# Dilated attention in pairs of query blocks, with the probabilities divided on VectorE and a new order of the first output products

## The chip, the cores and the metric

The kernel runs on one core of a Trainium2 chip. TensorE (PE) multiplies matrices out of SBUF into PSUM, VectorE (DVE), ScalarE (ACT) and GpSimd (POOL) work on tiles, and SyncE (SP) issues the DMA transfers. Each engine has its own queue, works it off in order, and waits on semaphores for the others. The metric is the device time of one execution in microseconds (us); less is better.

## What is computed

One layer of a hybrid decoder, for 1024 positions of width 1024, all in float32. Cut to what matters here:

```python
h = rmsnorm(x, norm1_w)
proj = h @ w_in                       # 3592 columns: q, k, v, gate z, b, a; then q, k, v of mixer B
...
o_a = gated_delta_rule(qa, ka, va, g, beta)        # mixer A: 4 heads of 128
o_a = rmsnorm(o_a, gdn_norm_w) * jax.nn.silu(z)
o_b = dilated_attention(qb, kb, vb)                # mixer B: 8 heads of 64
x = x + jnp.concatenate([o_a, o_b], axis=-1) @ w_out
h = rmsnorm(x, norm2_w)
u = causal_dwconv(h @ w_up, ffn_conv_w)
x = x + (jax.nn.silu(gate) * up) @ w_down
return rmsnorm(x, final_norm_w)
```

`dilated_attention` has three branches, (window, dilation) = (128, 1), (512, 4), (2048, 16). In each, position t sees t, t-d, t-2d, ... back to t-window. The branches are merged by their softmax denominators, which is the same as one softmax over all the keys of the three branches, a key counting as often as it is in a branch.

## The kernel before, in words

**Layout.** Activations lie transposed: features on the partitions, the 1024 positions on the free axis, in two halves of 512. Float32 products are made of three products in fp32r, high by high, high by low and low by high (`mm3`, L184; `split`, L190, makes the high part on ScalarE and the low part, the difference, on VectorE). A weight tile of 128 columns (`weight`, L194) is loaded, and split into `whi` and `wlo`.

**Stages.** The input projection comes as *dense* columns (`dense`, L462): 128 output columns each, two halves, 24 products of 128x512 a half, then an evacuation out of PSUM that also applies the norm (`xr`, or `aqkv` for mixer B, which is parked in DRAM as `apark`). The list `DENSE` (L37) gives their order. In between run mixer A's chunked recurrence and, from 313 us on, mixer B's attention. Then follow the output projection (`out_proj`, L1003), the convolutional MLP, and the last norm; those after the output projection are not touched.

**Who sets the order.** Every stage is a Python generator, and a planner (`Weave`, L42) runs them all while the program is being built. It keeps a modelled time for TensorE (`pe`) and for each other engine, with an estimate for each operation: `mm(..., us)` (L176) gives a product's time, an `Engine` (L117) works out its own from the tile's size, and `account` (L74) notes when a tile will be ready. A generator yields how long it still has to wait (`need`, L91: the latest `ready` of its tiles minus `pe`, plus a slack), and the planner goes on with the most urgent stream (lowest level number) whose wait is over. Attention is at level 5, the output projection at 8, the dense columns at 9: a dense product goes to TensorE whenever attention's operands are, in the model, not ready. TensorE's order is pinned in the order in which the planner issues; the order of the other engines' queues is left to the tile scheduler. So an estimate moves instructions but has no time itself.

**Attention** (`attention`, L839) takes four pairs of heads (`pi` 0 to 3), two halves of 512 queries each (`hh`), four blocks of 128 queries in each half. Both heads of a pair go side by side, as they have 64 rows each. `att_load` (L816) loads q, k and v; `att_values` (L822) transposes v into `vn` (positions on the partitions) and makes `vc` from it by 16 DMA transfers, in which the positions are sorted by their class modulo 4. For one block of queries:

- `scores` (L856): two products of the *band*, 128 queries by up to 256 keys (the block and the one before it), and eight of the *window*, in tiles of 32 queries of one class by the keys of that class, 32 a block. The softmax rows are 256 wide for block 0 of a pair, 384 for blocks 1 to 3, 512 for blocks 4 to 7. Then, on the other engines: a masked reduction to the negative maximum (`sm<-ps,mk`, VectorE), `exp` with its sum (`sm<-sm,mx`, ScalarE), the reciprocal of the sums (`mx<-mx`, VectorE), and the division, a multiplication by it (`sm<-sm,mx` again, ScalarE).
- `turn` (L887): transposes of the probabilities through PSUM. The band's part is copied to `pt` (VectorE), the window's part to `pb` (ScalarE).
- `values` (L900): products of `vn` and `pt` into the half's bank `po`.
- `merge_classes` (L908), once in a half: products of `vc` and the `pb` of all four blocks into the same bank. `give` (L920) then copies `po` out; the halves go to DRAM (`mixer`), the last one stays in SBUF as `oT`.

`advance` (L935) puts blocks into a pipe. With block i's scores issued, it issues the values of block i-2 (and the classes and `give` when that was a half's last) and then the turn of block i-1.

PSUM has 8 banks: the tags `hf`, `asc`, `ch` and `atr` have two each (`bank`, L226). Scores take `asc`, turns `atr`, `po` is in `ch`, dense products in `hf`. Tiles with a tag ending in `*` take turns between two tags (`A`, L156): `dv*` means `dv` and `dw`, two buffers each, where the `sm` lie; `t1` has three buffers, for `pt` (and two tiles of other stages, L305 and L618).

**The output projection.** `mixer_splits` (L978) loads the eight head blocks of the mixers' output (four of mixer A, already gated in SBUF; four of mixer B, from DRAM) and splits them into `ohi` and `olo`; the tag of the loaded tile, `ev`, has two buffers and is shared with the gate of the last dense columns. `out_proj` (L1003) has the output tiles in the order of `MORDER`; for the first two, in four banks, it goes over the head blocks outside and the two tiles inside; from the third on a tile is one run of 8 head blocks a half. Two weight tiles are held at a time.

Of the kernel before, what the change touches and what calls it, by code (L numbers as in the profile page):

```python
# [15 lines left out]
P = 128  # L16
# [17 lines left out]
HOP = 0.5  # L34
ASLACK = 1.2
MSLACK = 1.5
MGAP = 0.6  # L37
DENSE = ([("k", 3), ("a", 0, 0), ("a", 0, 1)] + [(c, h) for h in range(4) for c in "qv"] + [("a", 0, 2)]
         + [("a", p, i) for p in (1, 2, 3) for i in range(3)] + [("z", h) for h in range(4)])
# [96 lines left out]
def hybrid_layer(tc, I, out):  # L136
# [14 lines left out]
    def tile_(pool, shape, dt, name, tag, bufs):  # L151
        return wv.slot(pool.tile(list(shape), dt, name=name, tag=tag, bufs=bufs), tag, bufs)
# [73 lines left out]
    def bank(tag, name="ps"):  # L226
        return tile_(pp_, (P, 512), F32, name, tag, 2)
# [10 lines left out]
    def v8(t):  # L238
        return t.rearrange("p (c t) -> p c t", c=NCH)
# [62 lines left out]
    dtb = const("dtb", [P, H], bass.AP(tensor=I["dt_bias"].tensor, offset=I["dt_bias"].offset, ap=[[0, P], [1, H]]))  # L302
    gw2 = const("gw2", [P, 1])
    ve.tensor_scalar(gw2, gnw, 0.5, None, op0=OP.mult)
    wba = tile_(sp, [P, KT, 32], F32, "wba", "t1", 3)  # L305
    po_.memset(wba, 0.0)
    sy.dma_start(wba[:, :, :8], I["wba"])
    ve.tensor_tensor(wba[:, :, :8], wba[:, :, :8], n1[:, :, None].to_broadcast([P, KT, 8]), op=OP.mult)
# [302 lines left out]
    def forward_sub():  # L611

        mt_t = A("mt", "go")
        sy.dma_start(mt_t, mdram.rearrange("h p f -> (h p) f"))
        mt = mt_t.rearrange("p (j i) -> p j i", j=32)
        xi_t = A("xi", "go")
        xi = xi_t.rearrange("p (i c) -> p i c", i=32)
        tmp = tile_(sp, [P, 256], F32, "tmp", "t1", 3)  # L618
# [203 lines left out]
    def att_values(vT):  # L822

        vn, vc = A("vn", "kt"), A("vc", "kt")
        for hh in range(2):
            pt = yield from next_bank("atr", vT, slack=ASLACK * (hh == 0))
            for c in range(4):
                i = 4 * hh + c
                tp(pt[:, c * P:(c + 1) * P], vT[:, i * P:(i + 1) * P])
            ac.activation(vn[:, half(hh)], pt, AF.Copy)  # L830
        for c in range(4):
            for n in range(4):
                sy.dma_start(vc[32 * n:32 * n + 32].rearrange("u (c b d) -> u c b d", c=4, b=2)[:, c],
                             vn[32 * c:32 * c + 32].rearrange("u (b n d) -> u n b d", b=2, n=4)[:, n])
        return vn, vc

    HALVES = (slice(0, 64), slice(64, 128))

    def attention():  # L839
# [13 lines left out]
            t = mks[i]  # L853
            return bass.AP(tensor=t.tensor, offset=t.offset + o, ap=[t.ap[0], [step, m], [1, w]]), m

        def scores(it):  # L856
            n, q, k, nb = it["n"], it["q"], it["k"], it["nb"]
            pss = [bank("asc") for _ in range(2)]
            yield wv.need(*pss, q, k)
            k0 = max(n - 1, 0) * P  # L860
            n1_, n2_ = (n + 1) * P - k0, P * nb
            wd = n1_ + n2_
            for e, er in enumerate(HALVES):
                mm(pss[e][:, :n1_], q[er, n * P:(n + 1) * P], k[er, k0:k0 + n1_], 0.0009 * n1_)
            for c in range(4):
                o = slice(32 * c, 32 * c + 32)
                for e, er in enumerate(HALVES):
                    mm(pss[e][o, n1_:wd].rearrange("p (n u) -> p n u", u=32), q[er, n * P + 32 * c:n * P + 32 * c + 32],
                       by_block(k)[er, :4 * nb, c, :], 0.00025 * n2_, tile_position=(64 * e, 32 * c))
            sm = A("sm", "dv*", shape=(P, 2, 512))  # L870
            mx = tile_(sp, [P, 4], F32, "mx", "mx", 4)
            mn, den = mx[:, :2], mx[:, 2:]
            mv, m = mask(n)
            for e in range(2):
                ve.tensor_tensor_reduce(out=sm[:, e, :wd].rearrange("p (a b) -> p a b", a=m),
                                        in0=pss[e][:, :wd].rearrange("p (a b) -> p a b", a=m), in1=mv, scale=-0.125,
                                        scalar=-NEG, op0=OP.add, op1=OP.min, accum_out=mn[:, e:e + 1])
            for e in range(2):
                ac.activation(sm[:, e, :wd], sm[:, e, :wd], AF.Exp, bias=mn[:, e:e + 1], scale=-1.0,
                              accum_out=den[:, e:e + 1])  # L880

            ve.reciprocal(den, den)
            for e in range(2):
                ac.activation(sm[:, e, :wd], sm[:, e, :wd], AF.Copy, scale=den[:, e:e + 1])
            it.update(sm=sm, wd=wd, n1=n1_, k0=k0)

        def turn(it):  # L887
            sm, wd, n1_ = it["sm"], it["wd"], it["n1"]
            it["pt"] = []
            for e in range(2):  # L890
                pt = tile_(sp, [P, 256], F32, "pt", "t1", 3)
                it["pt"].append(pt)
                pp = bank("atr")
                yield wv.need(pp, sm)
                for i in range(wd // P):
                    tp(pp[:, i * P:(i + 1) * P], sm[:, e, i * P:(i + 1) * P])
                ve.tensor_copy(pt[:, :n1_], pp[:, :n1_])
                ac.activation(it["pb"][e][:, it["u"]].rearrange("p b t -> p (b t)"), pp[:, n1_:wd], AF.Copy)

        def values(it):  # L900
            u = it["u"]
            yield wv.need(it["po"], *it["pt"])
            for i in range(it["n1"] // P):
                for e, er in enumerate(HALVES):
                    mm(it["po"][er, u * P:(u + 1) * P], v8(it["vn"])[:, it["k0"] // P + i, er],
                       it["pt"][e][:, i * P:(i + 1) * P], 0.12, u == 0 and i == 0, False, skip_group_check=True)

        def merge_classes(g):  # L908
            vcv = g["vc"].rearrange("p (c b d) -> p c b d", c=4, b=2)
            po, nb = g["po"], g["nb"]  # L910
            yield wv.need(*g["pb"])
            for c in range(4):
                for b in range(nb):
                    for e in range(2):
                        er = slice(64 * e, 64 * e + 64)
                        mm(po[er].rearrange("p (u t) -> p u t", u=4)[:, :, 32 * c:32 * c + 32],
                           vcv[:, c, b, er], g["pb"][e][:, :, b, 32 * c:32 * c + 32], 0.14,
                           False, c == 3 and b == nb - 1, skip_group_check=True)
# [13 lines left out]

        pipe = []

        def advance(it):  # L935
            if it is not None:
                yield from scores(it)
            pipe.insert(0, it)
            if len(pipe) > 2:
                done = pipe.pop()  # L940
                if done is not None:
                    yield from values(done)
                    if done["u"] == 3:
                        yield from merge_classes(done["g"])
                        give(done["g"])
            if len(pipe) > 1 and pipe[1] is not None:
                yield from turn(pipe[1])

        for pi in range(4):
            q, k, vn, vc = cur  # L950
            for hh in range(2):
# [9 lines left out]
                for u in range(4):  # L961
                    yield from advance(dict(n=4 * hh + u, u=u, q=q, k=k, vn=vn, nb=nb, po=po, pb=pb, g=g))
            if pi < 3:
                cur = qkv[:2] + (yield from att_values(qkv[2]))
        for _ in range(2):
            yield from advance(None)


    ots = {}
# [33 lines left out]
    def out_proj():  # L1003
# [2 lines left out]
        yield from wv.until("last group")  # L1006
        yield from wv.until("residual")
        pts = {m: [bank(t) for _ in range(2)] for m, t in zip(MORDER, ("hf", "ch"))}
        for k in range(8):
            yield from wv.until(("ot", k))  # L1010
            for m, w in zip(MORDER, ws):
                for h in range(2):
                    yield wv.need(pts[m][h], *w, *ots[k])
                    mm3(pts[m][h], [t[:, k, :] for t in w], [t[:, half(h)] for t in ots[k]], k == 0, k == 7)
        for j, m in enumerate(MORDER):
            w = ws.pop(0)
            for h in range(2):
# [468 lines left out]
```

## Time and profile before

| | us |
|---|---|
| median of 3 runs (lowest, highest) | 1257.34 (1256.65, 1259.51) |
| profiled execution | 1259.56 |
| span in its trace, first to last instruction | 1257.8 |
| granted TensorE clock, mean | 0.993 of full speed |

The stretch that the change touches, from the trace's table by windows (busy us of each engine, with the number of instructions):

| from : to, us | PE | DVE | ACT | POOL | DMA share |
|---|---|---|---|---|---|
| 315.8 : 515.8, attention | 199.5 (1754) | 107.8 (268) | 117.1 (278) | 0 | 0.25 |
| 515.8 : 538.3, first two output tiles | 22.4 (97) | 12.6 (16) | 9.2 (13) | 0 | 0.42 |

Busy time of PE is the time in which at least one matmul is under way, and matmuls are pipelined: a stretch that is filled may still hold time in which no column moves. So stalls of TensorE are read here from the starts of its instructions. In the tables and views, a name such as `sm<-ps,mk` is the tile written and the tiles read, L132 is the line of the helper through which every operation of VectorE, ScalarE and GpSimd goes, L177 that of `mm` and L181 that of the transposes; x64 is the number of instructions in a group. A tile's shape is partitions by elements.

Attention's own work on its tiles, from the trace's view of one tile (ns; lowest, median, highest):

| instruction | engine | count | ns |
|---|---|---|---|
| `sm<-ps,mk` reduction, two forms | DVE | 32 and 32 | 398, 687, 701 and 540, 558, 692 |
| `sm<-sm,mx`, 64 `exp` and 64 divisions | ACT | 128 | 496, 664, 731 |
| `ps<-ident,sm` transposes | PE | 216 | 270, 273, 330 |
| `pt<-ps` copies | DVE | 64 | 270, 421, 436 |
| `ps<-pt,vn` value products | PE | 240 | 272, 273, 323 |

### The profile page before, as it was taken

What the parts mean: (1) busy time and instruction counts of PE and PEld (TensorE: products, weight loads), DVE (VectorE), ACT (ScalarE), POOL (GpSimd) and SP (SyncE); (2) the same over time, 40 slices, a digit from 0 to 9 for tenths busy, and PEclk for the clock granted to TensorE, in tenths of its full rate; (3) what the DMA queues carried; (4) which work ended last, traced back from release to release, by engine and by line L of the source; (5) the groups of instructions that cost most, each with busy time, mean ns of one, the idle gap of its engine ahead of it and who ended that gap; (6) DMA issues with size and microseconds to landing.
All of it is one profiled execution on the core that took longest, in us unless ns stands there. A gap on an engine that the chain in (4) does not pass through costs nothing.

```text
span 1257.8 us, 18320 instructions
## 1 busy us (share of the span) xinstructions
PE 1233.0 (98%) x7040; PEld 1002.1 (80%) x7040; DVE 936.0 (74%) x1462; ACT 621.8 (49%) x1179; POOL 47.8 (4%) x34
## 2 busy tenths in 40 slices
PE   9989999999999999999999999999999999999996
PEld 7768887888676767878788888888888888787886
DVE  7566975563555455676798888888988989899875
ACT  7374444462757374465554454544544454343451
POOL 0021110022000000000000000000000000000000
PEclk9989999999999999999999999999999999999998
DMA  6313244255223420454312313223223298545523
GB/s 228 100 57 94 85 116 137 101 160 206 96 78 100 140 63 26 126 179 139 118 51 101 92 59 101 85 67 101 79 73 101 68 353 290 167 138 198 192 85 134
DMA packets 81974, 153.52 MB, mean 122 GB/s; under 512 B 21824, under 2 KB 32736, under 8 KB 81888
## 3 DMA queue, kind: packets, MB, share of 16 engines
q1 hardware_dynamic: 81888, 152.37, 37.1%
q8 instruction: 55, 0.90, 0.3%
q14 instruction: 31, 0.25, 0.1%
HBM read 114.31 MB, written 35.93 MB: 119 GB/s over the span
## 4 chain that ended last, share of the span: by engine, by line
PE 84%; DVE 7%; DMA 4%; ACT 2%; issue 2%; SPq 0%; POOL 0%; POOLq 0%; DVEq 0%; ACTq 0%
PE ps L177 44%; PE pa L177 18%; PE pc L177 9%; PE dw L177 8%; PE ps L181 4%; DMA wd<-in_wd 3%; DVE pr L132 2%; DVE x1h L132 1%; DVE wd L132 1%; ACT dec L132 1%; DVE kT L132 1%; PE warm L177 1%; DMA wst<-in_wu 0%; DVE r L132 0%; DVE xr L132 0%
## 5 line engine op out<-in xcount | busy, mean ns | idle before, releaser
L177 PE MATMUL dw<-pr 128*128 128x512 f32 (+1 forms) x984 | 213.3, 377 | 2.8 <-DVE x1h L132 2.8
L177 PEld LDWEIGHTS dw<-pr 128*128 128x128 f32 x984 | 176.1, 188 | 38.9 <-DVE x1h L132 4.9
L177 PE MATMUL ps<-xhi,whi 128*128 128x512 f32 x448 | 186.5, 416 | 0.0
L177 PE MATMUL ps<-xhi,wlo 128*128 128x512 f32 x448 | 175.8, 392 | 0.0
L177 PE MATMUL ps<-xlo,whi 128*128 128x512 f32 x448 | 175.3, 391 | 0.0
L177 PE MATMUL pa<-T,pair 128*128 128x512 f32 x528 | 127.1, 389 | 0.6 <-ACT u L132 0.6
L177 PEld LDWEIGHTS pa<-T,pair 128*128 128x128 f32 x528 | 99.0, 188 | 21.1 <-ACT u L132 0.7
L177 PEld LDWEIGHTS ps<-xhi,whi 128*128 128x128 f32 x448 | 84.6, 189 | 19.9 <-issue 6.0
L177 PEld LDWEIGHTS ps<-xhi,wlo 128*128 128x128 f32 x448 | 84.4, 188 | 18.5
L177 PEld LDWEIGHTS ps<-xlo,whi 128*128 128x128 f32 x448 | 84.8, 189 | 13.5
L132 ACT ACTIVATE sm<-sm,mx 128x512 f32<-128x512 f32 (+2 forms) x128 | 79.9, 651 | 23.0 <-DVE mx L132 23.0
L132 ACT ACTIVATE u<-pa 128x512 f32<-128x512 f32 x44 | 26.4, 600 | 110.5 <-PE pa L177 110.5
L132 DVE SCALAR_TENSOR_TENSOR y<-xu,fcw,y 128x1023 f32<-128x1023 f32 (+1 forms) x44 | 56.3, 1281 | 25.7 <-ACT y L132 25.7
L132 ACT ACTIVATE whi<-wst 128x1024 fp32r<-128x1024 f32 (+2 forms) x38 | 38.7, 1017 | 70.4 <-PE ps L177 63.0
L177 PE MATMUL pc<-B,pair 128*128 128x512 f32 x264 | 63.4, 389 | 0.0
L177 PE MATMUL pa<-B,A 128*128 128x512 f32 x264 | 63.4, 389 | 0.0
L177 PE MATMUL pc<-T,S 128*128 128x512 f32 x264 | 63.4, 389 | 0.0
L177 PE MATMUL pa<-T,S 128*128 128x512 f32 x264 | 63.4, 389 | 0.0
L132 ACT ACTIVATE pr<-wd 128x1024 fp32r<-128x1024 f32 x33 | 35.0, 1061 | 55.0 <-DVE wd L132 36.5
L132 DVE TENSOR_TENSOR wst<-wst 128x512 f32<-128x512 f32 x88 | 60.5, 687 | 0.7
L177 PE MATMUL ps<-B,pair 128*128 128x512 f32 x252 | 60.5, 389 | 0.0
L177 PEld LDWEIGHTS pc<-B,pair 128*128 128x128 f32 x264 | 49.6, 188 | 10.3
(230 smaller groups left out, 2279.8 us busy)
## 6 DMA issues: line engine op xcount, KB each, us to landing
wst<-in_wu SPq DMA_DIRECT2D x44, 512.0 KB, 3.7
wd<-in_wd SPq DMA_DIRECT2D x44, 512.0 KB, 4.3
wst<-in_wi SPq DMA_DIRECT2D x25, 512.0 KB, 3.7
upark<-y SPq DMA_DIRECT2D x22, 512.0 KB, 3.7
apark<-aqkv SPq DMA_DIRECT2D x12, 512.0 KB, 2.8
r<-upark SPq DMA_DIRECT2D x11, 512.0 KB, 7.6
r<-upark SPq DMA_DIRECT2D x22, 256.0 KB, 6.7
wa<-in_wd SPq DMA_DIRECT2D x22, 256.0 KB, 2.9
```

Source lines behind the costliest of these rows:

```text
L132: return getattr(eng, op)(*a, **kw)
L177: tc.stamp_issue_order_token(nc.tensor.matmul(dst, lhs, rhs, start=start, stop=stop, **kw).ins, TOKEN)
L181: tc.stamp_issue_order_token(nc.tensor.transpose(dst, src, ident).ins, TOKEN)
```

## The change

1. **Pairs of blocks.** `scores`, `turn` and `values` take two blocks at a time. The first block's scores and turns use the banks `asc`, the second's `atr`. Within `scores`, the band products of both blocks come first, then the window products of both; the same operations as before on the other engines are put in a function of their own, `softmax`, once a block. The pipe is one pair deep: `advance` issues the turn of the pair before, the scores of the new pair, the values of the pair before, and its classes. Values and classes are offered 0.5 us before the model has their operands ready (`PSLACK`), turns 0.2 us after (`TSLACK`); some estimates of products are lower. The four `pt` of a pair are one tile in `dv*`.
2. **`vc` estimate.** The planner takes `vc` as ready 6.0 us after `vn`, whatever it had summed up for the 16 transfers.
3. **Division on VectorE.** `tensor_scalar` by the reciprocal on VectorE in the place of ScalarE's activation: 64 instructions from one queue to the other.
4. **First output tiles by heads.** For the first two output tiles, the head blocks 0 to 6 of the first tile, then those of the second, then block 7 of both.
5. **`t1`** keeps one buffer, for the two tiles of other stages.

TensorE's program has the same 6002 instructions in both kernels.

```diff
+PSLACK = 0.5
+TSLACK = 0.2, 0.2
...
-    wba = tile_(sp, [P, KT, 32], F32, "wba", "t1", 3)
+    wba = tile_(sp, [P, KT, 32], F32, "wba", "t1", 1)
...
+        wv.ready[vc.tensor.name] = max(wv.pe, wv.ready[vn.tensor.name]) + 6.0
         return vn, vc
...
-        def scores(it):
+        def scores(pair):
+            for it, tag in zip(pair, ("asc", "atr")):
...
+                it["ps"] = [bank(tag) for _ in range(2)]
+            yield wv.need(*pair[0]["ps"], *pair[1]["ps"], pair[0]["q"], pair[0]["k"])
+            for it in pair:
+                n, k0, n1_ = it["n"], it["k0"], it["n1"]
                 for e, er in enumerate(HALVES):
+                    mm(it["ps"][e][:, :n1_], it["q"][er, n * P:(n + 1) * P], it["k"][er, k0:k0 + n1_], 0.00085 * n1_)
+            for it in pair:
+                n, n1_, wd = it["n"], it["n1"], it["wd"]
+                for c in range(4):
+                    o = slice(32 * c, 32 * c + 32)
+                    for e, er in enumerate(HALVES):
+                        mm(it["ps"][e][o, n1_:wd].rearrange("p (n u) -> p n u", u=32),
+                           it["q"][er, n * P + 32 * c:n * P + 32 * c + 32], by_block(it["k"])[er, :4 * it["nb"], c, :],
+                           0.00022 * (wd - n1_), tile_position=(64 * e, 32 * c))
+                softmax(it)
...
             ve.reciprocal(den, den)
             for e in range(2):
-                ac.activation(sm[:, e, :wd], sm[:, e, :wd], AF.Copy, scale=den[:, e:e + 1])
...
+                ve.tensor_scalar(sm[:, e, :wd], sm[:, e, :wd], den[:, e:e + 1], None, op0=OP.mult)
+
+        def turn(pair):
+            pts = A("pt", "dv*", shape=(P, 4, 256))
+            for b, (it, tag) in enumerate(zip(pair, ("asc", "atr"))):
...
+                    pt = pts[:, 2 * b + e, :]
+                    it["pt"].append(pt)
+                    pp = bank(tag)
+                    yield wv.need(pp, sm, slack=TSLACK[b])
+                    for i in range(wd // P):
+                        tp(pp[:, i * P:(i + 1) * P], sm[:, e, i * P:(i + 1) * P])
+                    ve.tensor_copy(pt[:, :n1_], pp[:, :n1_])
...
+        def values(pair):
+            yield wv.need(pair[0]["po"], *pair[0]["pt"], slack=-PSLACK)
+            for it in pair:
+                u = it["u"]
+                for i in range(it["n1"] // P):
                     for e, er in enumerate(HALVES):
...
+                           it["pt"][e][:, i * P:(i + 1) * P], 0.11, u == 0 and i == 0, False, skip_group_check=True)
...
-            yield wv.need(*g["pb"])
+            yield wv.need(*g["pb"], slack=-PSLACK)
...
-        def advance(it):
...
-            if len(pipe) > 2:
-                done = pipe.pop()
...
-            if len(pipe) > 1 and pipe[1] is not None:
-                yield from turn(pipe[1])
+        def advance(pair):
+            done = pipe.pop() if pipe else None
+            if done is not None:
+                yield from turn(done)
+            if pair is not None:
+                yield from scores(pair)
+                pipe.append(pair)
+            if done is not None:
+                yield from values(done)
+                if done[1]["u"] == 3:
+                    yield from merge_classes(done[0]["g"])
+                    give(done[0]["g"])
...
-        for k in range(8):
+
+        for k, j in [(k, j) for j in range(2) for k in range(7)] + [(7, 0), (7, 1)]:
             yield from wv.until(("ot", k))
-            for m, w in zip(MORDER, ws):
-                for h in range(2):
-                    yield wv.need(pts[m][h], *w, *ots[k])
-                    mm3(pts[m][h], [t[:, k, :] for t in w], [t[:, half(h)] for t in ots[k]], k == 0, k == 7)
+            m, w = MORDER[j], ws[j]
+            for h in range(2):
+                yield wv.need(pts[m][h], *w, *ots[k])
+                mm3(pts[m][h], [t[:, k, :] for t in w], [t[:, half(h)] for t in ots[k]], k == 0, k == 7)
```

More of the change, by code (lines that the diff above doesn't have):

```diff
@@ L617, in forward_sub @@
         xi = xi_t.rearrange("p (i c) -> p i c", i=32)
-        tmp = tile_(sp, [P, 256], F32, "tmp", "t1", 3)
+        tmp = tile_(sp, [P, 256], F32, "tmp", "t1", 1)
         po_.memset(xi, 0.0)
@@ L854, in mask @@
             return bass.AP(tensor=t.tensor, offset=t.offset + o, ap=[t.ap[0], [step, m], [1, w]]), m
-        def scores(it):
[L857 to L866, printed above, removed]
-                for e, er in enumerate(HALVES):
-                    mm(pss[e][o, n1_:wd].rearrange("p (n u) -> p n u", u=32), q[er, n * P + 32 * c:n * P + 32 * c + 32],
-                       by_block(k)[er, :4 * nb, c, :], 0.00025 * n2_, tile_position=(64 * e, 32 * c))
-            sm = A("sm", "dv*", shape=(P, 2, 512))
+        def scores(pair):
+            for it, tag in zip(pair, ("asc", "atr")):
+                it["k0"] = max(it["n"] - 1, 0) * P
+                it["n1"] = (it["n"] + 1) * P - it["k0"]
+                it["wd"] = it["n1"] + P * it["nb"]
+                it["ps"] = [bank(tag) for _ in range(2)]
+            yield wv.need(*pair[0]["ps"], *pair[1]["ps"], pair[0]["q"], pair[0]["k"])
+            for it in pair:
+                n, k0, n1_ = it["n"], it["k0"], it["n1"]
+                for e, er in enumerate(HALVES):
+                    mm(it["ps"][e][:, :n1_], it["q"][er, n * P:(n + 1) * P], it["k"][er, k0:k0 + n1_], 0.00085 * n1_)
[8 more added lines that the diff above has]
+                softmax(it)
@@ L871, in scores, with softmax @@
+        def softmax(it):
+            pss, wd = it.pop("ps"), it["wd"]
+            sm = it["sm"] = A("sm", "dv*", shape=(P, 2, 512))
             mx = tile_(sp, [P, 4], F32, "mx", "mx", 4)
             mn, den = mx[:, :2], mx[:, 2:]
-            mv, m = mask(n)
+            mv, m = mask(it["n"])
             for e in range(2):
@@ L883, in scores @@
             for e in range(2):
-                ac.activation(sm[:, e, :wd], sm[:, e, :wd], AF.Copy, scale=den[:, e:e + 1])
[L885 to L906, printed above, removed]
+                ve.tensor_scalar(sm[:, e, :wd], sm[:, e, :wd], den[:, e:e + 1], None, op0=OP.mult)
@@ new lines, in turn @@
+        def turn(pair):
+            pts = A("pt", "dv*", shape=(P, 4, 256))
+            for b, (it, tag) in enumerate(zip(pair, ("asc", "atr"))):
+                sm, wd, n1_ = it["sm"], it["wd"], it["n1"]
+                it["pt"] = []
+                for e in range(2):
+                    pt = pts[:, 2 * b + e, :]
[5 more added lines that the diff above has]
+                    ve.tensor_copy(pt[:, :n1_], pp[:, :n1_])
+                    ac.activation(it["pb"][e][:, it["u"]].rearrange("p b t -> p (b t)"), pp[:, n1_:wd], AF.Copy)
@@ L908, in merge_classes @@
+        def values(pair):
[3 more added lines that the diff above has]
+                for i in range(it["n1"] // P):
+                    for e, er in enumerate(HALVES):
+                        mm(it["po"][er, u * P:(u + 1) * P], v8(it["vn"])[:, it["k0"] // P + i, er],
+                           it["pt"][e][:, i * P:(i + 1) * P], 0.11, u == 0 and i == 0, False, skip_group_check=True)
         def merge_classes(g):
@@ L933, in attention @@
         pipe = []
-        def advance(it):
-            if it is not None:
-                yield from scores(it)
-            pipe.insert(0, it)
-            if len(pipe) > 2:
-                done = pipe.pop()
[L941 to L945, printed above, removed]
-            if len(pipe) > 1 and pipe[1] is not None:
-                yield from turn(pipe[1])
+        def advance(pair):
[10 more added lines that the diff above has]
+                    give(done[0]["g"])
         for pi in range(4):
@@ L960, in attention @@
                 g = dict(po=po, pb=pb, nb=nb, hh=hh, pi=pi, vc=vc)
-                for u in range(4):
-                    yield from advance(dict(n=4 * hh + u, u=u, q=q, k=k, vn=vn, nb=nb, po=po, pb=pb, g=g))
+                for u in (0, 2):
+                    yield from advance([dict(n=4 * hh + i, u=i, q=q, k=k, vn=vn, nb=nb, po=po, pb=pb, g=g)
+                                        for i in (u, u + 1)])
             if pi < 3:
                 cur = qkv[:2] + (yield from att_values(qkv[2]))
-        for _ in range(2):
-            yield from advance(None)
+        yield from advance(None)
     ots = {}
```

## The prediction

> **What bounds the kernel now.** I read the page first, then the waits and the timeline of the attention stage, because the diff touches nothing outside it but the order of the first output products.
>
> ```profile
> span 1257.8 us, 18320 instructions
> ...
> PE 1233.0 (98%) x7040; PEld 1002.1 (80%) x7040; DVE 936.0 (74%) x1462; ACT 621.8 (49%) x1179; POOL 47.8 (4%) x34
> ...
> PE 84%; DVE 7%; DMA 4%; ACT 2%; issue 2%; SPq 0%; POOL 0%; POOLq 0%; DVEq 0%; ACTq 0%
> ```
>
> TensorE is the bound: 98% busy, 84% of the chain. The stage runs from the first head pair's value transposes (313.48) to the first output product (515.84), 202.4 us. Who TensorE waited for in it:
>
> ```profile
> PE ps L177 <- ACT pb L132: 0.2, 1, 0.2
> PE ps L177 <- DVE mx L132: 0.2, 1, 0.2
> ```
>
> So engines cost it 0.4 us there. What costs it is changing tile shape, which no view names. TensorE's timeline (start, length) of two blocks:
>
> ```profile
> 326.47 1.08 PE L177 MATMUL ps<-kT,qT 64*128 64x256 f32 x20
> 327.48 0.50 PE L177 MATMUL ps<-xhi,whi 128*128 128x512 f32 x1
> ...
> 330.52 1.29 PE L177 MATMUL ps<-kT,qT 64*128 64x256 f32 x20
> 331.75 0.66 PE L177 MATMUL ps<-pt,vn 128*64 128x128 f32 x8
> 332.34 0.50 PE L177 MATMUL ps<-xhi,whi 128*128 128x512 f32 x1
> ```
>
> The starts tell: a score group lasts 1.01 us and, with twice the window part, 1.23. So the short window part is 0.22, the band part about 0.42 (a 128-column band group is 0.21 shorter), and 0.37 is left that no column explains: about 0.21 between the band and the window shape, 0.17 on the way out. Value products lose 0.16 on the way out: 331.75 to 332.34 is 0.59, 0.43 of it work.
>
> VectorE and ScalarE serve one block like this (two views):
>
> ```profile
> 331.91 0.69 DVE L132 CUSTOM_DVE_ANT_1 sm<-ps,mk 128x512 f32<-128x512 f32 x1 [0.85 <-PE ps L177]
> 332.53 0.08 DVE L132 DVE_READ_ACCUMULATOR2_ANT mx<- 128x1 f32 x1
> ...
> 334.06 1.06 DVE L132 TENSOR_TENSOR aqkv<-ps,rstdB 128x512 f32<-128x512 f32 x1 [0.83 <-PE ps L177]
> 334.95 0.16 DVE L132 RECIPROCAL mx<-mx 128x2 f32<-128x2 f32 x1
> ```
> ```profile
> 332.64 0.73 ACT L132 ACTIVATE sm<-sm,mx 128x512 f32<-128x512 f32 x1 [1.27 <-DVE mx L132]
> ...
> 333.37 0.71 ACT L132 ACTIVATE sm<-sm,mx 128x512 f32<-128x512 f32 x1
> ```
>
> Reductions follow each other every 0.62 us, exponentials every 0.71, and the first exponential starts 0.73 after its reduction. A dense evacuation (aqkv) sits in VectorE's queue between a block's reduction and its reciprocal; nobody waits, since a block is turned only after the next one's scores.
>
> **Step 1, pairs: switches saved.** I counted the switches of TensorE's queue in both kernels and priced each at its median excess over work in the trace. Band to window 32 to 16 at 0.21: -3.4. Out of scores 32 to 16 at 0.17: -2.7. Out of values to anything but classes 24 to 8 at 0.16: -2.6. Dense to values 11 to 1 at 0.22: -2.2. Transposes to scores 15 to 1 at 0.15: -2.1. Dense to probability transposes 12 to 25 at 0.14: +1.8. Small ones: -0.4. Stalls of before above these medians: -1.4. Sum **-13.0 us**, to 189.4. The two blocks inside a group count as free: values with 4 records (323.86 to 324.23, 0.37) and with 8 (0.59) differ by their work alone. If a block inside a group paid both inner prices, 16 x 0.38 = 6 us would come back; that end goes into the range.
>
> **Step 2, the divide moves to VectorE.** 64 divides leave ScalarE (the second half of the x128 group at 651 ns; 38 us) and join VectorE, which was busy 107.8 of 200 us there; neither load decides, the latency does. The trace has no such divide with both ends in SBUF. From below, the shortest copy in the stage, 0.28 us for 128 columns; from above 0.68, a TENSOR_SCALAR of 512 columns out of PSUM (683 ns). I take 0.68, the same operation at the same length (0.55 and 0.42 for 384 and 256, like the reductions). Then in a pair of 512 columns, counted from the first reduction: four reductions 2.46, the reciprocal 0.25, the divide 0.68 and a 0.1 hop: the first block can be turned 3.5 us after it, its second head 0.17 after TensorE wants it. Pairs with blocks 0 and 1 need 2.4.
>
> [...]
>
> **Step 3, what TensorE waits for now.** With one pair in flight, turn follows scores and values of the same round, and the dense products between them are the cover. Where the cover is whole (9 to 30 dense products, 2 to 7 us) there is no wait. Where it is not, VectorE's queue decides, for the evacuation of a dense half (next one 1.0 us later) and the low part of a weight (1.14) stand ahead of the first reduction, and the dense half ends just as the scores begin:
> - Blocks 4 and 5 of head pairs 0 and 1. VectorE: 0.2 + 1.0 + 1.14 + 3.5 = 5.85 us after the dense half. TensorE: entry 0.19, scores 2.1, values 1.0, classes 1.0 and their switches, no dense: 4.0. Wait 1.85 + 0.17, twice: 4.0.
> - Blocks 0 and 1 of head pairs 1 and 2: 2.35 + 2.4 = 4.75 against 4.2 (both class halves): 0.5 + 0.15, twice: 1.3.
> - The last pair of head pair 2. Ahead of its reductions stand xr (0.69), wlo and the gate zz (3.4 us with the start), and og (1.14) is inside: 3.4 + 1.23 + 1.14 + 1.25 + 1.0 = 8.0 against 4.7: 3.4.
> - The last scores of head pair 3 need banks whose pb copies stand behind whi and zz on ScalarE (1.06 each): 1.4.
> - The last turn: two olo of 1.2 stand ahead of the last pt copies: 1.3.
> - The first pair (aqkv between the two divides): 0.8.
>
> Sum **+12.2 us**. Attention: -13.0 + 12.2 = -0.8.
>
> **Step 4, first output tiles.** The last dense product ends at 515.84 (call it E), and ots follow on VectorE:
>
> ```profile
> 516.04 0.69 DVE L132 TENSOR_TENSOR xr<-ps,rstdB 128x512 f32<-128x512 f32 x1 [0.39 <-PE ps L177]
> ...
> 521.71 1.23 DVE L132 TENSOR_TENSOR olo<-og,ohi 128x1024 fp32r<-128x1024 f32 x1 [1.13 <-ACT ohi L132]
> 523.90 0.69 DVE L132 TENSOR_TENSOR olo<-ot,ohi 128x512 fp32r<-128x512 f32 x1 [0.97 <-ACT ohi L132]
> 525.38 2.03 DVE L132 TENSOR_TENSOR olo<-ot,ohi 128x512 fp32r<-128x512 f32 x3 [0.78 <-ACT ohi L132]
> ...
> 530.75 1.45 DVE L132 TENSOR_TENSOR olo<-ot,ohi 128x512 fp32r<-128x512 f32 x2
> ```
>
> Head block 3 is ready at E+7.1, block 6 at E+15.6 (its first half of the x2 row, 531.43); those loads wait for buffers that the gate frees, and the changed queues keep that order. Before, TensorE spends 12 products of 0.227 a block, wants block 3 at E+8.2 and block 6 at E+16.3, and finishes all 96 at E+22.5. After, it spends 6 a block, wants block 3 at E+4.1 and block 6 at E+8.2, stands until E+16.1, and has 42 + 12 products left: 12.2 us, E+28.3. **+5.8 us.** The stall on the third tile's wlo (0.93 at 539.72) stays, as the same two products precede it.
>
> **Step 5.** The vc estimate and the t1 buffers only reorder: class products still come over 15 us after their 16 transfers begin, and GpSimd is idle in the stage. 0, at most 1 either way.
>
> **Sum**: -0.8 + 5.8 = +5.0 us on the profiled execution's 1259.56 (span 1257.8), which stands 2.2 above the median; on the median 1257.34 that is **1262.4 us**.
>
> **Rivals.**
> - *VectorE is in time (faster).* If the evacuations of the first three places of step 3 are done before the scores end, their 8.7 us go and the sum is -3.7: 1253.6. It turns faster by over 0.2% once these waits cost less than about 1.2 us together. For it: 0.4 us of such waits before, and a divide at half my price. Against it: the queue order. 0.18.
> - *They cancel.* These waits half as long, since every stall lets VectorE catch up: +0.7, 1258. 0.20.
> - *The joint groups save no switch inside.* +6: 1268.4. Against it the 4- and 8-record values. 0.10, part of slower; the forecast itself has 0.52.
>
> The chance of slower by over 0.2% (2.5 us, about what a measurement of this kernel can tell from no change) is 0.62, within 0.20, faster 0.18. The range runs from the first rival to the third, 1253.5 to 1268.
>
> **What would show it.** Score groups near 1.9 us for two short blocks and half as many switches (step 1); a divide group x64 on VectorE at 0.4 or 0.68 (step 2); TensorE waiting for sm on VectorE, 8 us or more, at head pair 2's end most (step 3); the first output products stretched from 22.5 to 28 us, waiting for olo and ohi (step 4). I am wrong if TensorE hardly waits for sm, or if block 6 comes sooner after E.

## The result, and the profile after

The changed kernel takes 1261.28 us, median of 20 runs, beside 1259.01 for the kernel before (20 runs, where the three ahead of the prediction had 1257.34). The ratio of the two sets of runs is 1.0022, with a 95% interval of 1.0016 to 1.0029, so the kernel is slower by 0.22%. The medians lie 2.3 us apart, where the forecast had 5.0; that is inside its range. That the change costs time is clear; whether it costs more than 0.2%, the line that the prediction drew, is not, since the interval begins below it. The profiled execution took 1262.77 us, 3.2 more than that of before. From its page:

```profile
span 1261.0 us, 18315 instructions
...
PE 1227.4 (97%) x7040; PEld 1007.6 (80%) x7040; DVE 958.1 (76%) x1526; ACT 585.6 (46%) x1115; POOL 48.1 (4%) x34
...
PE 82%; DVE 9%; DMA 4%; ACT 3%; issue 3%; SPq 0%; POOL 0%; POOLq 0%; DVEq 0%; ACTq 0%
```

TensorE is 5.6 us less busy in a span that is 3.2 longer: it does the same 7040 products and waits more. In the chain's shares, DVE went from 7% to 9% and PE from 84% to 82%.

I cut the span at instructions that both programs have, read off TensorE's timeline: the first value transposes of attention, the first output product, the first product of the third output tile.

| us | before | after | difference |
|---|---|---|---|
| start to first value transposes | 313.5 | 313.9 | +0.4 |
| value transposes to first output product | 202.4 | 198.8 | **-3.6** |
| first two output tiles (96 products) | 22.5 | 29.9 | **+7.4** |
| third tile to the end | 719.5 | 718.4 | -1.1 |

The last row is the same work in both kernels. In the profiled executions below, its long part after the last output product ran from 650.2 to 654.2 us, so the 1.1 is scatter. What is to be explained is a gain of 3.6 and a loss of 7.4.

**Attention.** TensorE's waits there (us in total, times, longest), 0.4 us before:

```profile
PE ps L183 <- DVE sm L134: 3.2, 4, 1.4
PE ps L183 <- DVE mx L134: 3.2, 1, 3.2
PE ps L179 <- ACT pb L134: 0.6, 1, 0.6
PE ps L179 <- DVE pt L134: 0.3, 1, 0.3
```

These are the idle times; the starts of the products give somewhat more, 8.7 us in all. Blocks 4 and 5 of the first head pair, TensorE's timeline (start, length), and VectorE's:

```profile
336.49 2.16 PE L179 MATMUL ps<-kT,qT 64*128 64x256 f32 x40
338.57 1.09 PE L179 MATMUL ps<-pt,vn 128*64 128x128 f32 x16
339.50 1.04 PE L179 MATMUL ps<-pb,vc 128*64 128x128 f32 x16
341.92 0.63 PE L183 MATMUL ps<-ident,sm 128*128 128x128 f32 x4 [1.38 <-DVE sm L134]
```
```profile
336.59 1.08 DVE L134 TENSOR_TENSOR aqkv<-ps,rstdB 128x512 f32<-128x512 f32 x1 [0.94 <-PE ps L179]
337.52 1.22 DVE L134 TENSOR_TENSOR wlo<-wst,whi 128x1024 fp32r<-128x1024 f32 x1
338.65 0.68 DVE L134 CUSTOM_DVE_ANT_1 sm<-ps,mk 128x512 f32<-128x512 f32 x1
...
341.09 0.16 DVE L134 RECIPROCAL mx<-mx 128x2 f32<-128x2 f32 x1
341.29 0.88 DVE L134 TENSOR_SCALAR sm<-sm,mx 128x512 f32<-128x512 f32 x2
```

The reader is to see the queue that step 3 described: an evacuation and a low part ahead of the first reduction, four reductions, the reciprocal, two divisions; and on TensorE scores, values and classes back to back with no dense product, and then the wait. The score group of both blocks is one row (x40), where before each block had its own.

The longest wait, at the last head pair's value transposes, and what it waits for, VectorE's reduction of the pair's second block, first head, and its read-out into `mx`:

```profile
449.91 1.97 PE L183 MATMUL ps<-ident,vT 128*128 128x128 f32 x8 [3.16 <-DVE mx L134]
```
```profile
449.17 0.68 DVE L134 CUSTOM_DVE_ANT_0 sm<-ps,mk 128x512 f32<-128x512 f32 x1
449.77 0.08 DVE L134 DVE_READ_ACCUMULATOR2_ANT mx<- 128x1 f32 x1
```

**First output tiles.** TensorE's timeline where head block 6 arrives:

```profile
526.32 0.50 PE L179 MATMUL ps<-ohi,whi 128*128 128x512 f32 x1 [1.44 <-ACT ohi L134]
527.05 0.50 PE L179 MATMUL ps<-olo,whi 128*128 128x512 f32 x1 [0.23 <-DVE olo L134]
...
528.25 0.80 PE L179 MATMUL ps<-olo,whi 128*128 128x512 f32 x1 [0.24 <-DVE olo L134]
528.85 0.63 PE L179 MATMUL ps<-ohi,wlo 128*128 128x512 f32 x1
529.27 0.63 PE L179 MATMUL ps<-ohi,whi 128*128 128x512 f32 x1
```

With E = 512.68, the end of the dense products, TensorE stands for block 3 at E+5.9 and E+7.1 and for block 6 until E+15.6, nearly as in step 4 (E+7.1 and E+16.1). But then come products 0.42 us apart, not 0.23. The trace's table by windows has the clock (PE busy, weight loads, DVE, ACT, POOL, granted clock, DMA share, GB/s):

```profile
516.00:528.20 12.20, 8.13 (x28) 4.54 (x26) 7.17 (x11) 5.89 (x9) 0.00 (x0) 0.99 0.60 193
528.20:531.40 3.20, 3.15 (x7) 2.51 (x8) 0.61 (x1) 0.00 (x0) 0.00 (x0) 0.50 0.00 0
531.40:540.00 8.60, 8.60 (x39) 7.11 (x38) 0.00 (x0) 0.00 (x0) 0.00 (x0) 1.00 0.00 0
```

By the trace's record of the granted clock, from which the table has its means, TensorE ran at half its clock from 528.00 to 531.41, which cost 1.6 us. The same happened in attention at the wait of 3.2 us, ahead of the last value transposes (449.49 to 452.91; the windows here are cut a little later):

```profile
446.00:449.80 3.80, 0.75 (x14) 0.51 (x10) 3.80 (x9) 1.52 (x4) 0.00 (x0) 0.96 0.47 138
449.80:453.00 3.20, 3.09 (x12) 2.71 (x13) 2.68 (x10) 2.57 (x6) 0.00 (x0) 0.51 0.02 5
```

The kernel before has no such place in these two stretches, and the prediction had no such term. A third stretch at half clock in the changed kernel, from 623.57 to 626.99, lies in the last row, which is the same work in both; of the 13 profiled executions in this document six have one there and seven, that of the kernel before among them, have none.

### The profile page after: what moved, and what is told of

Same layout as the page of the kernel before. It is cut to its first block, busy times and chain, and to the rows that moved or that the text cites. A ratio compares the mean times of both kernels' runs of the same rounds, so it can differ in the third digit from the quotient of the medians.

```text
span 1261.0 us, 18315 instructions
## 1 busy us (share of the span) xinstructions
PE 1227.4 (97%) x7040; PEld 1007.6 (80%) x7040; DVE 958.1 (76%) x1526; ACT 585.6 (46%) x1115; POOL 48.1 (4%) x34
## 4 chain that ended last, share of the span: by engine, by line
PE 82%; DVE 9%; DMA 4%; ACT 3%; issue 3%; SPq 0%; POOL 0%; POOLq 0%; DVEq 0%; ACTq 0%
PE ps L179 41%; PE pa L179 19%; PE pc L179 9%; PE dw L179 9%; PE ps L183 3%; DMA wd<-in_wd 2%; DVE pr L134 2%; DVE wd L134 1%; DVE x1h L134 1%; DVE sm L134 1%; DVE wlo L134 1%; ACT dec L134 1%; DMA ot<-mixer 1%; DVE kT L134 1%; PE warm L179 1%
## 5 line engine op out<-in xcount | busy, mean ns | idle before, releaser
L134 ACT ACTIVATE sm<-sm,mx 128x512 f32<-128x512 f32 (+2 forms) x64 | 41.2, 645 | 43.9 <-DVE mx L134 43.9
L179 PEld LDWEIGHTS pa<-T,S 128*128 128x128 f32 x264 | 49.5, 188 | 10.3
```

The lines of the kernel that those rows point to most:

```text
L134: return getattr(eng, op)(*a, **kw)
L179: tc.stamp_issue_order_token(nc.tensor.matmul(dst, lhs, rhs, start=start, stop=stop, **kw).ins, TOKEN)
```

## The experiments

Theory A: the pairs gain what they save in changes of tile shape, less waits for VectorE's chain; the new order of the first tiles loses 5.8 us in waits; and the half clock comes from the standing. All ratios are to the kernel before, timed on the same chip; "attention" and "first tiles" are the second and third row of the table above, each from one profiled execution (the time of extra products, where a kernel has some, is in them).

| kernel | ratio, 95% interval | attention | first tiles |
|---|---|---|---|
| before | 1 | 202.4 | 22.5 |
| changed | 1.0022 (1.0016 to 1.0029) | 198.8 | 29.9 |
| e1 changed, old order of first tiles | 0.9968 (0.9957 to 0.9980) | 198.9 | 22.5 |
| e2 before, new order of first tiles | 1.0051 (1.0039 to 1.0063) | 202.3 | 29.8 |
| e3 changed, divisions on ScalarE | 1.0079 (1.0066 to 1.0092) | 206.0 | 28.6 |
| e4 before, divisions on VectorE | 1.0000 (0.9990 to 1.0009) | 202.1 | 22.5 |
| e5 changed, scores block by block | 1.0028 (1.0015 to 1.0040) | 200.2 | 27.8 |
| e6 changed, filled first tiles | 1.0027 (1.0016 to 1.0037) | 198.8 | 28.4 |
| e7 e1, more cover for one wait | **0.9946** (0.9932 to 0.9960) | 195.2 | 22.5 |
| e8 changed, no `vc` estimate | 1.0021 (1.0009 to 1.0034) | 200.0 | 28.5 |
| e9 e1, that wait filled | 0.9955 (0.9938 to 0.9972) | 197.5 | 22.5 |
| e10 changed, again | 1.0020 (1.0009 to 1.0032) | 197.5 | 29.8 |
| e11 e6, again | 1.0018 (1.0010 to 1.0027) | 198.7 | 28.1 |

**e1 and e2: the order of the first tiles, taken out and put in alone.**

```diff
 # e1, on the changed kernel (e2 is the reverse, on the kernel before)
-        for k, j in [(k, j) for j in range(2) for k in range(7)] + [(7, 0), (7, 1)]:
+        for k in range(8):
...
+            for m, w in zip(MORDER, ws):
```

> The changed kernel with the first two output tiles in the old order (head blocks outside, both tiles inside); TensorE's program up to the first output product is that of the changed kernel. Theory A (the order of the first tiles costs 7.4 us, the pairs gain 3.6): the first 96 output products take 22.5 us again, not 29.9; the span falls by 7.4 to about 1253.6 and the ratio to the kernel before is 0.996 to 0.998. Rival R1 (the head blocks are late because attention in pairs ends with its engines behind, whatever the order): the 96 products still take over 26 us, and the ratio stays above 0.999.

> The kernel before with the new order of the first output tiles and nothing else. Theory A: the 96 products take 28 us, the 5.8 of the prediction's step 4, and up to 30 if TensorE's clock halves after the waits as it does in the changed kernel; ratio 1.004 to 1.006. R1: 22.5 to 24 us, ratio within 0.001 of 1.

Both came out as theory A has it: 22.5 and 29.8 us. R1 falls: the old order has no wait in these tiles even after attention in pairs. The order alone costs 0.5%, and the pairs without it are 0.3% faster than the kernel before.

**e3 and e4: the divisions.** The planner's account stays as it was, so TensorE's order is that of the changed kernel (e3) or of the kernel before (e4).

```diff
 # e3 (e4 is the reverse, on the kernel before)
-                ve.tensor_scalar(sm[:, e, :wd], sm[:, e, :wd], den[:, e:e + 1], None, op0=OP.mult)
+                wv.account("vector", 0.07 + 0.00105 * wd, [sm], [sm, den], 0.28)
+                nc.scalar.activation(sm[:, e, :wd], sm[:, e, :wd], AF.Copy, scale=den[:, e:e + 1])
```

> The changed kernel with the 64 divisions back on ScalarE, while the planner still counts them on VectorE, so that TensorE's order is that of the changed kernel. Theory A (the pairs' waits come from the whole chain reduction, exp, reciprocal, division, and the division is the short end of it on VectorE): ScalarE has four exponentials of 0.71 and then the divisions of 0.69 in one queue, so a pair is ready 0.7 to 1.4 us later than the changed kernel's, at the seven places that wait now: value transposes to first output product 200 to 204 us, not 198.8. Rival R4 (VectorE, with 28 us more of work, is what makes the pairs late): the waits shrink, below 198, and the kernel is faster than the changed one.

> The kernel before with the 64 divisions on VectorE and TensorE's order as it was. Theory A (two blocks in flight cover the chain whichever engine divides): value transposes to first output product 202.4 us within 1, ratio within 0.001 of 1. R4: more than 1.5 us longer.

e3 went A's way and beyond its 204: 206.0. ScalarE's timeline of the pair shown above, in e3:

```profile
339.99 0.72 ACT L134 ACTIVATE sm<-sm,mx 128x512 f32<-128x512 f32 x1 [1.94 <-DVE mx L134]
...
342.82 2.54 ACT L899 ACTIVATE sm<-sm,mx 128x512 f32<-128x512 f32 x4
```

All four divisions stand behind all four exponentials, so TensorE turns the first probabilities at 343.58, 3.6 us after the first exponential's start, where it took 2.5 with VectorE (339.44 to 341.92 in the changed kernel). TensorE waits 8.8 us for ScalarE's `sm` at 7 places, in place of 3.2 at 4. e4 is within 0.3 us of before. So R4 falls: in the pairs the move to VectorE saves 7.2 us (206.0 less 198.8), and with two blocks in flight it is worth nothing.

**e5: is a change of shape inside a group free?** The matmuls are issued band, window, band, window; the planner counts as before.

```diff
+            for b in range(2):
+                for dst, lhs, rhs, us, kw in bands[b] + wins[b]:
+                    tc.stamp_issue_order_token(nc.tensor.matmul(dst, lhs, rhs, start=True, stop=True, **kw).ins, TOKEN)
```

> The changed kernel, with the band and window products of a pair's first block ahead of those of its second (band, window, band, window), all else in the planner's order as it is. Theory A (a change of tile shape costs 0.21 us into the window and 0.17 out of it, in a group as well as between groups): 16 pairs pay 0.38 more, +6.1 us on the changed kernel, less at most 1 us because the first block's reduction can start sooner; value transposes to first output product 204 us, not 198.8. Rival R2 (what a switch costs is the start of a group, not the shape): no change, within 1 us of the changed kernel.

A miss of both. The changes of shape are there at the price expected: 16 more into the window at 0.21 and 16 more out of it at 0.17, 5.9 us by the starts. But attention is only 1.4 us longer, as the first block's reduction starts sooner and TensorE arrives later: the wait at the value transposes fell from 3.2 to 1.7 and took the half clock with it, that of the two pairs after the classes from 1.4 to 1.1 each. (Beside e10, the changed kernel in an execution without that half clock, attention is 2.7 us longer.) R2 falls by the rows, not by the time, which is within 1 us of the changed kernel's, and so does the expectation's 6.1: of the 5.9 us added on TensorE ahead of its waits for VectorE, attention shows 1.4.

**e6, e9, e10, e11: the half clock.** e6 and e11 are one kernel: 12 extra products into a spare bank ahead of blocks 3 and 6 of the first tile. e9 puts 12 ahead of the last value transposes. What they add up is not used.

```diff
+        FILL = {(3, 0, 0): 5, (6, 0, 0): 6, (6, 0, 1): 1}
+        spare = bank("asc")
...
+                for _ in range(FILL.get((k, j, h), 0)):
+                    tc.stamp_issue_order_token(nc.tensor.matmul(spare, w[0][:, 0, :], ots[0][0][:, half(0)], ...
```

> The changed kernel with 12 extra products of 128x512 into a bank that nobody reads, 5 ahead of head block 3 and 7 ahead of head block 6 of the first output tile, where TensorE waits. They add work and no result. Theory A (the half clock from 528 to 531 us comes from the waits ahead of it): the clock stays at 1.0, the 96 products take 28.3 us, not 29.9, and the kernel is 1.6 us faster than the changed one. Rival R3 (the half clock has another cause): the clock is 0.5 there again and the time is the same, or longer by what the 12 products do not hide, up to 2.7.

> The first experiment's kernel (old order of the first output tiles) with 12 extra products of 128x512 into a bank that nobody reads, just ahead of the last head pair's value transposes, where TensorE stands 3.2 us for VectorE. They add 2.7 us of work and no result, and the wait itself stays. Theory A (the half clock behind that wait comes from the standing): the clock stays 1.0, the 8 transposes take 1.0 us and not 1.95, value transposes to first output product 197.3 us, not 198.9, and the time is up to 1.6 us lower than the first experiment's. Rival R3 (the clock falls for another reason): 198.9, with the clock at 0.5 there.

> The changed kernel once more, timed beside the next one on the same chip. Theory A: ratio to the kernel before 1.002 again, and 1.0 to 1.6 us longer than the next kernel. If the half clock in the first output tiles is rare and the profiled execution had it by chance, the two agree within 0.5 us.

> The kernel with 12 extra products in the first output tiles once more: its trace showed the wait's half clock gone (28.4 us, not 29.9) but its time, on another chip run, no gain. Theory A: 1.0 to 1.6 us faster than the changed kernel beside it. Rival (the half clock comes only in some executions, or the extra products cost elsewhere what they save): equal within 0.5 us, or slower.

Where the wait was filled, the clock stayed at 1.0, in all three: e6 and e11 have 28.4 and 28.1 us for the first tiles, e9 has 197.5 for attention (its time, 1254.44 us, cannot be told from e1's). From e9, the windows to be laid beside those of the changed kernel above:

```profile
446.00:449.80 3.80, 3.80 (x28) 2.79 (x24) 3.80 (x7) 1.53 (x4) 0.00 (x0) 1.00 0.50 142
449.80:453.00 3.20, 2.98 (x22) 2.57 (x22) 3.09 (x12) 2.49 (x6) 0.00 (x0) 1.00 0.00 0
```

But e10, the changed kernel itself in another execution, has the same wait and no half clock behind it:

```profile
445.50:449.20 3.70, 0.57 (x12) 0.33 (x6) 3.70 (x9) 1.52 (x4) 0.00 (x0) 1.00 0.51 142
449.20:452.50 3.30, 3.27 (x22) 2.81 (x23) 3.18 (x10) 2.71 (x7) 0.00 (x0) 1.00 0.02 5
```

So in these places the half clock needs the standing, as far as three fills can show, but the standing does not always bring it: the wait of 3.2 us was followed by it in five profiled executions of six (changed, e1, e3, e6, e11; not e10).

In the times, the fill of the first tiles gained nothing that can be told: e11 and e10, side by side, have medians of 1261.76 and 1261.69. The expected 1.0 to 1.6 us is not there. It is not that the half clock is rare: all six profiled executions with the new order and no fill have it in these tiles (changed, e2, e3, e5, e8, e10). But in e3, e5 and e8, which differ from the changed kernel in attention alone, it falls between the arrivals of blocks 3 and 6, where the time that it costs would otherwise have been spent waiting for block 6. From e5, whose products of block 6 begin at 526.67:

```profile
521.20:524.60 3.40, 3.40 (x10) 2.63 (x9) 2.71 (x4) 2.09 (x4) 0.00 (x0) 0.50 0.40 141
```

Those three take 28.6, 27.8 and 28.5 us, about as long as with the fill, and the three in which it falls behind the arrival of block 6 (changed, e2, e10) take 29.8 to 29.9. So the fill can gain only in some executions. How many of the timed ones these are, and whether the extra products cost something elsewhere, the runs don't tell.

**e7: the version that the experiments point to.** e1, and the planner offers the last head pair's value transposes 3.4 us later.

```diff
-    def att_values(vT):
+    def att_values(vT, slack=ASLACK):
...
-            pt = yield from next_bank("atr", vT, slack=ASLACK * (hh == 0))
+            pt = yield from next_bank("atr", vT, slack=slack * (hh == 0))
...
-                cur = qkv[:2] + (yield from att_values(qkv[2]))
+                cur = qkv[:2] + (yield from att_values(qkv[2], ((1.2, 1.2, 4.6))[pi]))
```

> The first output tiles in the old order as in the first experiment, and one more edit: the planner offers the value transposes of the last head pair 3.4 us later, so that 12 dense products stand ahead of them where TensorE stood 3.2 us and then ran 3 us at half clock; these products come out of later, longer runs of dense products. Theory A (that wait and the half clock behind it cost 4.8 us, and cover is free where it is taken): the wait falls under 0.7, the clock stays 1.0, value transposes to first output product 194 to 195 us, ratio to the kernel before 0.993. Rival R5 (dense products are the only cover and all are in use, so the wait turns up where they are taken from): 198 to 199 us as in the first experiment, ratio 0.996 to 0.998.

Attention takes 195.2 us, 3.7 less than in e1: the wait fell to 0.2 of idle time and the clock stayed up; some 0.5 us of new waits at the turns behind it are what is missing of the expected 194 to 195. Theory A, then, not R5. With 1251.78 us it is the fastest kernel here, 0.5% below the kernel before, where 0.7% was expected; its interval overlaps that of e1 a little, and that of e9 in great part.

**e8: the `vc` estimate.**

```diff
-        wv.ready[vc.tensor.name] = max(wv.pe, wv.ready[vn.tensor.name]) + 6.0
```

> The changed kernel without the line that sets when the planner takes vc as ready. The planner then has TensorE standing for vc in its model and puts no dense products between the classes and the next turn, for all four head pairs, and 33 at the end of attention, not 9. My prediction's step 5 (the estimate only reorders): within 1 us of the changed kernel. Theory B (the estimate is worth what it covers): the turns behind the classes of the first half wait 3.0 us at four places, 12 in all and not 2.9, while the wait of 3.2 for the value transposes and its half clock go: about 4 us slower than the changed kernel, 2 to 6.

The time is the changed kernel's, as my step 5 had it, but not for its reason. TensorE's timeline behind the classes of the first half:

```profile
342.49 1.06 PE L183 MATMUL ps<-ident,sm 128*128 128x128 f32 x8 [1.37 <-DVE sm L134]
344.58 1.59 PE L183 MATMUL ps<-ident,sm 128*128 128x128 f32 x8 [1.02 <-DVE sm L134]
```

Both turns wait, 2.5 us together, at four places: 10 us where theory B had 12, against 2.9 in the changed kernel; a half clock follows the first of them (1.3). What comes back is the wait at the value transposes with its half clock (4.6), those of blocks 0 and 1 (0.6), of the last scores (1.2) and of the last turn (0.7): +1.3 by this sum, +1.2 measured. Theory B's 4 was a miss, as it left the smaller returns out. The estimate decides where the dense products stand, and one place costs about what the other does.

## Why the prediction was right, step by step

- **What bounds it.** Right: TensorE's own queue, with changes of shape as the hidden cost.
- **Step 1, -13.0.** About -13.7, as what is left of the whole. By the starts, excess over work between the first scores and the first output product was 27.9 us before and 24.3 after; 8.7 of the latter are waits and 1.4 the half clock, so 14.2 are left for switches, 13.7 less than the 27.9. e5 shows that the groups' inner switches were rightly counted as saved.
- **Step 2.** The mechanism was right, the price was not: a division took 0.48, 0.42 and 0.35 us for 512, 384 and 256 columns, the next one starting 0.40 after the first, and not 0.68, 0.55 and 0.42. The row of 0.68 that I took reads PSUM (683 ns for 512 columns); the division has both ends in SBUF. From 256 to 512 columns it grows by 0.13 us, 0.52 ns a column. The 0.4 that the prediction's last line sets beside 0.68 rests on no row of before; the runs showed the 0.48, 0.42 and 0.35. A division at half my price, which the first rival leans on, would be 0.34: 512 columns took 0.71 of my price.
- **Step 3, +12.2.** This is the mis-sized term: 8.7. By place, forecast and measured: blocks 4 and 5, 4.0 and 2.9; blocks 0 and 1, 1.3 and 0.6; last pair of head pair 2, 3.4 and 3.2; bank of the last scores, 1.4 and 1.2; last turn, 1.3 and 0.7; first pair, 0.8 and 0.1. All six are there. The first is 0.6 shorter each time: the chain from the first reduction took 3.3 and not 3.5, it began 0.25 sooner after the dense half, and the second head needed no further wait. The third stands ahead of the value transposes, whose bank still held the unreduced scores, and not ahead of the probabilities. The queue of VectorE there was forecast rightly (xr, the low part, the gate, `og` inside), the instruction that waits for it was not, so that 3.2 came near 3.4 is luck.
- **Step 4, +5.8.** 5.9 and 5.6 in e6 and e11, where the clock stayed up; +7.4 in the changed kernel, +7.3 alone (e2). The waits were right; the missing term is the half clock, 1.6 in these executions and nothing that can be told in e3, e5 and e8.
- **Step 5, 0.** Right in size for the `vc` estimate (e8), for the wrong reason. The buffers of `t1` and the slacks (`PSLACK`, `TSLACK`) were not tried apart.
- **Sum.** -13.7 + 8.7 + 1.4 = -3.6, and 5.8 + 1.6 = +7.4: +3.8, where I had -0.8 + 5.8 = +5.0. Waits 3.5 too dear, switches 0.7 too cheap, half clock of 3.0 left out. As the switches are a remainder, that the sum closes proves nothing; that it came near the forecast is partly luck, since the two large errors have opposite signs. The 20 runs have +2.3; part of the half clock, which e10 lacks in one place and which cost e3, e5 and e8 nothing in another, may be the difference, but that was not measured.
- **Rivals.** VectorE was not in time (8.7 us of waits), so the first falls. The second wanted the first three places at half my 8.7, which is 4.4; they came to 6.7, about midway, and in time +2.3 lies about midway between its +0.7 and my +5.0. By size it is not ruled out. By its mechanism it falls for blocks 4 and 5: VectorE stood idle for 0.94 us ahead of the queue shown above, so it had nothing to catch up with, and what is shorter there is the chain. The third falls by e5's rows.

## What to carry to other kernels

When a change joins several edits, price each at its own place in the bounding engine's queue: here one edit paid for itself (0.3%) and another cost 0.5%, and the whole hid both. A loop order over operands that arrive one by one should use each operand for all the work that is waiting for it before it asks for the next: here 12 products a block hid the arrivals (22.5 us), 6 did not (29.9). And here extra work ahead of a wait was cheap (5.9 us more of it in e5, attention 1.4 longer), while work that covers a wait was scarce; so look where a planner has put its filler, and move it to the longest wait.

## What the runs showed of the hardware

By the clock records, TensorE's clock fell to 0.50 at waits in these places, and was at 1.00 again 3.41 us later (528.00 to 531.41 in the changed kernel): at the value transposes with one gap of 3.2 us; in the first tiles of the changed kernel after gaps of 1.4 and 0.2 with products between; in e8, from 345.0, after gaps of 1.4 and 1.0 with transposes between. Each of these cost 1.3 to 1.6 us, at most about half of the 3.41. Ahead of a wait it cost nothing that can be told (28.6, 27.8 and 28.5 us for the first tiles in e3, e5 and e8, beside 28.4 and 28.1 in e6 and e11, where the clock stayed at 1.0), and one execution of the same program, e10, escaped it at the value transposes.

What decides whether the clock falls isn't shown. In the changed kernel TensorE was busy, as the views count it, for 0.67 us of the 3.41 ahead of 449.49, for 1.75 of those ahead of 528.00 and for 2.76 of those ahead of 623.57, and each time the half clock came. In e10 it was busy for 0.57 us of 445.50 to 449.20, and it did not. Nor does the length of one gap tell: the longest single gap in the first tiles ahead of 528.00 was 1.44 us and in e8 ahead of 345.0 it was 1.37, and the half clock followed, while e10's 3.16 went without. One more regularity stands in the records of the changed kernel: its three stretches begin at 449.49, 528.00 and 623.57, which are 23 and 28 times 3.413 us apart. What sets these places, no run here shows.

Changes of tile shape cost TensorE 0.17 to 0.21 us each in scores, inside a group as between groups (e5). The views of waits do not count them as idle time (0.4 us in attention before); they show only in the starts.
